# A one-core transformer layer with 32 experts on Trainium2: three embedding tiles computed in plain float32 beside the routing, the weights of experts 2 and 3 loaded behind the first two gathers, gate and up weights in 4 KB runs

## The chip, the core and the metric

The kernel runs on one core of a Trainium2 chip. The metric is the device time of one execution in microseconds, as the median of several runs. Engines are named as in the profile: PE is TensorE, ACT ScalarE, DVE VectorE, POOL GpSimd, SP SyncE; SPq and POOLq are the issuing of DMAs by the last two.

## The reference, cut to what matters

One layer over 1024 tokens of 1024 features in float32. What the change touches is the part from the router on:

```python
x = x + concat([attn_out, ml_out]) @ w_o                     # mixers, output projection
x = x + _hier_moe(_rmsnorm(x, norm_ffn_g), ...)              # 32 experts, each token in 2 of them
hp = _rmsnorm(x, norm_ple_g)
x = x + (p @ w_ple) * sigmoid(hp @ w_ple_gate)               # p: 1024 x 256, w_ple: 256 x 1024
return _rmsnorm(x, final_norm_g)

# in _hier_moe, for the rows xb of one expert e (w_g, w_u: 1024 x 256; w_d: 256 x 1024):
(silu(xb @ w_g[e]) * (xb @ w_u[e])) @ w_d[e]
```

The product `p @ w_ple` depends on inputs alone, so it can be computed at any time before the last stage; it is the "embedding" of the text.

## The kernel before, in words

Tokens are cut into 8 tiles of 128. First come the mixers (0 to some 430 us), then `out_tile` for each tile: output projection (`wops`), the residual `xres`, the normalised rows `h`, their transposes (`h2p`, `h2t`) and router logits (`rps`). `h` and `xres` are stored to DRAM by POOL (`h2d`, `x2d`). `route_tiles` and `route_static` turn the logits on DVE into positions, counts (`cnt`) and a table (`tab`) that holds for each expert the rows to gather (`gidx`) and to scatter (`sidx`).

The expert loop (`experts`) goes over 32 experts. For each: a gather of its rows by indirect DMA on POOL (`xg`, filled ahead by ACT, `moe_setup` L1200), transposes (`xgp`), a split of them in two parts (`xh` on ACT, `xl` on DVE), 24 matmuls against gate and up (`gups`), their product (`eh`), its transposes (`ehp`, `eht`), 12 matmuls against down (`eyps`), and an indirect scatter (`ybd`). Nearly all products are made in three passes (`mm3`, L127 to L129) from operands that `split` cuts in a high and a low part, ACT writing the one (L132) and DVE the other (L133).

Expert weights are 3 MB each, as three transfers of 1 MB into a ring of raw slots (`R`, `rring`), two of gate and up (`rgu`, each as a gate and an up DMA of 512 KB, `load_gu`) and one of down (`rdn`, `load_dn`); then they are split into a second ring (`W`, `wring`). SP issues them in program order, and each waits until its slot is free. Experts 0 and 1 are loaded during `out_tile`, expert 2 at the end of it on SP, the gate and up of expert 3 on POOL around the first two gathers.

An embedding tile (`ple_tile`) takes a 128 x 256 piece of `p` (`pin`, loaded by `ple_in` on SP one or two experts ahead), transposes it (`pps`), splits it (`eht`), makes 12 matmuls of 512 columns (`pleps`) and two copies by ACT into the tile's result. Six tiles are made in the expert loop, at the experts in `PLE_AT`; their results lie in raw slots that `retire` takes out of the ring. Tile 6 comes behind the last expert in `final_load`, ahead of a loop for overflowing experts that is passed without work here, tile 7 behind that loop in `final`, which adds everything up.

A scheduler sets the order of the instructions on each engine from the program's order, dependences and priorities.

Of the kernel before, what the change touches and what calls it, by code (L numbers as in the profile page):

```python
# [20 lines left out]
P = 128  # L21
# [18 lines left out]
PLE_AT = (14, 16, 18, 20, 22, 24)  # L40
# [19 lines left out]
class Kernel:  # L60
# [64 lines left out]
    def mm3(self, out, w_hi, w_lo, m_hi, m_lo, start, stop):  # L125
# [3 lines left out]
        nc.tensor.matmul(out, w_lo, m_hi, start=False, stop=stop)  # L129
# [735 lines left out]
    def out_tile(self, i, gb, before):  # L865
# [14 lines left out]
        def mm(c, lo_k, hi_k):  # L880
            s = slice(c * 512, (c + 1) * 512)
            for k in range(lo_k, hi_k):
                self.mm3(ps[c], hi[:, k], lo[:, k], self.wo[k][:, 0, s], self.wo[k][:, 1, s], k == 0, k == KT - 1)
# [226 lines left out]
    def load_gu(self, e, b, q=None):  # L1110
        raw = self.R("rgu")
        v = raw.rearrange("p (k u f) -> p k u f", k=4, u=2)
        for u, n in enumerate(("w_gate_e", "w_up_e")):
            w = self.weight(n, e).rearrange("(p k) f -> p k f", k=KT)
            (q or self.nc.sync).dma_start(v[:, :, u, :], w[:, 4 * b:4 * b + 4, :])
        return raw

    def load_dn(self, e):
        raw = self.R("rdn")
        self.nc.sync.dma_start(raw, self.weight("w_down_e", e).rearrange("(p k) n -> p (k n)", k=2))  # L1120
        return raw
# [21 lines left out]
    def split_gu(self, raws):  # L1143
        return [(h[:, o:o + 512], l[:, o:o + 512]) for h, l in self.split_w(raws) for o in (0, 512)]
# [58 lines left out]
    def experts(self, gu3):  # L1203
        col = lambda t, e: t[:, e:e + 1]
        xg = [self.moe_gather(col(self.gidx, e)) for e in range(2)]
        with self.tc.issue_after(self.gathered.ins):
            self.raws[3] = gu3, self.load_gu(3, 1, self.nc.gpsimd), self.load_dn(3)
        x, gu, h, dn = {0: self.moe_x(xg[0])}, {0: self.first[0]}, {}, {0: self.first[1]}
        for e in range(N_EXP + 1):
# [24 lines left out]
            if e in PLE_AT:  # L1234
                self.ple_tile(PLE_AT.index(e))
            if e + 1 in PLE_AT[1:]:
                self.ple_in(PLE_AT.index(e + 1))

# [15 lines left out]
    def final_load(self):  # L1254
# [6 lines left out]
        for i in range(len(PLE_AT), NT):  # L1261
# [5 lines left out]
        with self.tc.issue_after(sa), self.tc.issue_after(sv):  # L1267
            self.wring, self.nw = wr, 0
            self.wgs = self.split_gate(raws[:1], 0)
            self.ple_tile(len(PLE_AT))  # L1270
            self.wgs += self.split_gate(raws[1:3], 2)
        self.rest = wr, raws[3:]
# [6 lines left out]
    def ple_load(self):  # L1279
# [3 lines left out]
        self.ple_in(0)  # L1283
# [17 lines left out]
    def ple_tile(self, i):  # L1301
# [7 lines left out]
        n = i - len(PLE_AT)  # L1309
        if n >= 0:  # L1310
            y = self.t("B", "pley", [P, D], bufs=2, tag="ey") if n % 2 else self.t("B", "pley", [P, D], tag=f"xg{n // 2 % 2}")
        else:
            if i % 2 == 0:
                pool, tag = self.retire()
                self.ples = self.t(pool, "ples", [P, 2 * D], tag=tag)
            y = self.ples[:, i % 2 * D:(i % 2 + 1) * D]
# [51 lines left out]
    def final(self):  # L1368
# [12 lines left out]
        rest = list(range(len(PLE_AT) + 1, NT))  # L1381
# [40 lines left out]
    def run(self):  # L1422
# [13 lines left out]
        for i in range(NT):  # L1436
            end = self.out_tile(i, gb, end)
            if i == 1:
# [62 lines left out]
```

## Time and profile before

| | us |
|---|---|
| median of 3 runs (1030.44 to 1032.11) | 1030.52 |
| the profiled execution | 1031.45 |
| its span in the profile | 1029.7 |
| mixers, about | 0 to 430 |
| `out_tile` and the routing behind it | 430 to 564 |
| expert loop, first `gups` to last `eyps` | 564 to 909 |
| last stage | 909 to 1029.7 |

The profiled execution has 1.75 us outside its span and its mean granted PE clock is 0.966. A row of the timeline has the start, the length, engine, line, operation, output and inputs, a count where several were merged, and in brackets how long the engine had been idle and what released it. Matmul lengths overlap, so the spacing is read from the starts.

### The profile page before, as it was taken

The numbers are of one execution on the slowest core, as the hardware profiler recorded it, in microseconds if no ns is written. First come the engines' busy times: TensorE is split into PE (matmuls) and PEld (weight loads), VectorE is DVE, ScalarE is ACT, GpSimd is POOL, SyncE is SP. The second block draws the span as 40 slices with busy tenths as digits, with TensorE's granted clock in tenths as the row PEclk, the third lists the DMA queues.
The fourth block names the chain that finished last, engine by engine and source line by source line (L and its number), as shares of the span: only waits on it lengthen the run. The fifth ranks groups of instructions, "written<-read, shape, count | busy, mean of one in ns | idle before, by whom it ended". The sixth has DMA issues, their size and how long they took to land. (4 is left out here: it accounts for less than half of the span.)

```text
span 1029.7 us, 16040 instructions
## 1 busy us (share of the span) xinstructions
PE 953.9 (93%) x5583; PEld 819.2 (80%) x5583; DVE 805.8 (78%) x1877; ACT 666.7 (65%) x1182; POOL 165.7 (16%) x213
## 2 busy tenths in 40 slices
PE   4999999998999999899995989999699999979996
PEld 4999999996788888688884867888588888858875
DVE  7759788367888989774747899998678889858885
ACT  5554766254788889763333877998578788755432
POOL 4000000101222322101013121222112112210000
PEclk9999999999999999899996998999899999989999
DMA  7230111310000001698348898999999999774541
GB/s 220 101 101 25 42 62 59 102 37 11 17 11 14 13 12 23 229 295 288 123 159 272 261 359 283 354 351 343 338 301 315 341 304 356 243 254 173 184 164 61
DMA packets 127360, 185.36 MB, mean 180 GB/s; under 512 B 19487, under 2 KB 105070, under 8 KB 123182
## 3 DMA queue, kind: packets, MB, share of 16 engines
q1 hardware_dynamic: 111502, 146.00, 42.4%
q0 software_dynamic: 15776, 38.33, 10.4%
q8 instruction: 44, 0.72, 0.3%
q14 instruction: 38, 0.31, 0.1%
HBM read 167.48 MB, written 33.59 MB: 195 GB/s over the span
## 5 line engine op out<-in xcount | busy, mean ns | idle before, releaser
L133 DVE TENSOR_TENSOR w<-rgu,w 128x1024 fp32r<-128x1024 f32 x128 | 155.1, 1227 | 32.8 <-ACT w L132 29.6
L132 ACT ACTIVATE w<-rgu 128x1024 fp32r<-128x1024 f32 x128 | 133.3, 1065 | 6.1 <-PE gups L129 3.3
L127 PE MATMUL inp<-hh,win 128*128 128x256 f32 x384 | 111.7, 291 | 0.0
L129 PE MATMUL inp<-hh,win 128*128 128x256 f32 x384 | 111.1, 290 | 0.5 <-DVE win L256 0.5
L128 PE MATMUL inp<-hl,win 128*128 128x256 f32 x384 | 111.4, 291 | 0.1
L127 PE MATMUL gups<-w,xh 128*128 128x512 f32 x256 | 103.8, 405 | 0.0
L128 PE MATMUL gups<-w,xh 128*128 128x512 f32 x256 | 102.0, 398 | 0.0
L129 PE MATMUL gups<-w,xl 128*128 128x512 f32 x256 | 101.2, 395 | 0.0
L133 DVE TENSOR_TENSOR w<-rdn,w 128x1024 fp32r<-128x1024 f32 x64 | 77.2, 1219 | 2.7 <-ACT w L132 1.9
L129 PEld LDWEIGHTS inp<-hh,win 128*128 128x128 f32 x384 | 74.6, 195 | 0.7 <-DVE win L256 0.7
L128 PEld LDWEIGHTS inp<-hl,win 128*128 128x128 f32 x384 | 74.6, 194 | 0.5 <-DVE hl L133 0.4
L127 PEld LDWEIGHTS inp<-hh,win 128*128 128x128 f32 x384 | 74.5, 194 | 0.3 <-ACT z L331 0.2
L132 ACT ACTIVATE w<-rdn 128x1024 fp32r<-128x1024 f32 x64 | 66.0, 1067 | 4.1 <-PE gups L129 3.7
L1149 POOL DMA_INDIRECT xg<-h2d,gidx x32 | 37.1, 1159 | 179.2 <-PE xgp L1159 145.8
L1188 ACT ACTIVATE ey<-eyps 128x512 f32<-128x512 f32 x64 | 38.2, 596 | 40.4 <-PE eyps L129 30.8
L705 PE MATMUL po<-pt,V 128*128 128x256 f32 x320 | 61.2, 307 | 0.9 <-ACT pt L132 0.5
L133 DVE TENSOR_TENSOR pt<-ptp,pt 128x512 fp32r<-128x512 f32 (+2 forms) x112 | 54.3, 491 | 7.3 <-ACT pt L132 5.7
L132 ACT ACTIVATE pt<-ptp 128x512 fp32r<-128x512 f32 (+2 forms) x112 | 48.1, 443 | 14.7 <-PE ptp L693 7.4
L127 PE MATMUL eyps<-w,eht 128*128 128x512 f32 x128 | 54.5, 426 | 2.4 <-ACT eht L132 2.3
L129 PEld LDWEIGHTS gups<-w,xl 128*128 128x128 f32 x256 | 48.3, 189 | 9.5
L128 PEld LDWEIGHTS gups<-w,xh 128*128 128x128 f32 x256 | 48.6, 190 | 9.1
L127 PEld LDWEIGHTS gups<-w,xh 128*128 128x128 f32 x256 | 48.7, 190 | 9.0 <-ACT xh L132 0.2
(392 smaller groups left out, 2633.2 us busy)
## 6 DMA issues: line engine op xcount, KB each, us to landing
rdn<-in_w_down_e_dram SPq DMA_DIRECT2D x32, 1024.0 KB, 8.9
rgu<-in_w_gate_e_dram SPq DMA_DIRECT2D x62, 512.0 KB, 11.5
rgu<-in_w_up_e_dram SPq DMA_DIRECT2D x62, 512.0 KB, 10.0
wraw<-in_w_in_dram SPq DMA_DIRECT2D x11, 512.0 KB, 5.4
x<-in_x_dram SPq DMA_DIRECT2D x8, 512.0 KB, 4.6
abw<-mlrows SPq DMA_DIRECT2D x8, 512.0 KB, 3.7
mixf<-mixd SPq DMA_DIRECT2D x8, 512.0 KB, 5.7
xres<-in_x_dram SPq DMA_DIRECT2D x8, 512.0 KB
```

The costliest lines, as they stand in the source:

```text
L127: nc.tensor.matmul(out, w_hi, m_hi, start=start, stop=False)
L128: nc.tensor.matmul(out, w_hi, m_lo, start=False, stop=False)
L129: nc.tensor.matmul(out, w_lo, m_hi, start=False, stop=stop)
L132: a = self.nc.scalar.activation(hi, src, AF.Copy)
L133: v = self.nc.vector.tensor_sub(lo, src, hi)
L705: nc.tensor.matmul(po, self.V[kt][:, h, :], pts[t - 1][:, w, u, :], start=(kt + w == 0), stop=(kt == 2 * j + 1 and w == 1))
L1149: self.gathered = self.nc.gpsimd.indirect_dma_start(out=xg, out_offset=None, in_=self.h2d, in_offset=bass.IndirectOffsetOnAxis(ap=gcol, ax ...
L1188: nc.scalar.activation(y[:, s], py[c], AF.Copy)
```

## The change

- Of the small edits left out of the diff, one keeps the last `wops` matmul as `last_out`. `early_in` loads `w_ple` as it is (1 MB) into a raw slot after the first `out_tile`; `early_p` loads the first three pieces of `p`; `early_tile` makes three embedding tiles in plain float32, without a split: 2 transposes, one ACT copy, 4 matmuls of 512 columns, two ACT copies, and a store of the result to DRAM by SP. They are issued behind the last `wops` matmul at a low priority. The result of the third lies in a slot of `xres`, which later is a slot of `W`.
- No embedding tile is left in the expert loop. At expert 26 `ple_back` loads the three results back into two retired raw slots. Tiles 3, 4 and 5 come in `final_load`, ahead of the overflow loop, tiles 6 and 7 in `final`.
- `load_gu` writes gate and up as 4 KB runs; before, runs of 1 KB alternated. `split_gu` reads and writes pieces of 256 elements, so that `W` holds what it held before.
- The loads of expert 2 and of expert 3 go on POOL's queue behind the first two gathers. The order of the raw ring shifts by one.

```diff
@@ -37 +37 @@
 MLPRI = 800
 PLE_LOAD = 5
 PLE_W = (7, 9)
-PLE_AT = (14, 16, 18, 20, 22, 24)
+N_EARLY = 3
+PLE_BACK = 26
 MAGIC = 12582912.0
 TWO_PI = 2.0 * math.pi
 C1 = 6.28125
...
@@ -1108 +1110 @@
         return w[e] if isinstance(e, int) else w[bass.ds(e, 1)].rearrange("o k f -> (o k) f")
     def load_gu(self, e, b, q=None):
         raw = self.R("rgu")
-        v = raw.rearrange("p (k u f) -> p k u f", k=4, u=2)
         for u, n in enumerate(("w_gate_e", "w_up_e")):
             w = self.weight(n, e).rearrange("(p k) f -> p k f", k=KT)
-            (q or self.nc.sync).dma_start(v[:, :, u, :], w[:, 4 * b:4 * b + 4, :])
+            (q or self.nc.sync).dma_start(raw[:, u * D:(u + 1) * D].rearrange("p (k f) -> p k f", k=4),
+                                          w[:, 4 * b:4 * b + 4, :])
         return raw
-    def load_dn(self, e):
+    def load_dn(self, e, q=None):
         raw = self.R("rdn")
-        self.nc.sync.dma_start(raw, self.weight("w_down_e", e).rearrange("(p k) n -> p (k n)", k=2))
+        (q or self.nc.sync).dma_start(raw, self.weight("w_down_e", e).rearrange("(p k) n -> p (k n)", k=2))
         return raw
     def split_w(self, raws):
...
@@ -1141 +1144 @@
         return out
     def split_gu(self, raws):
-        return [(h[:, o:o + 512], l[:, o:o + 512]) for h, l in self.split_w(raws) for o in (0, 512)]
+        out = []
+        side = lambda t: t.rearrange("p (k u f) -> p u k f", k=2, u=2)
+        for raw in raws:
+            v = raw.rearrange("p (u k f) -> p u k f", u=2, k=4)
+            for j in range(2):
+                hi, lo = self.W("w")
+                self.last_split = self.split(side(hi), side(lo), v[:, :, 2 * j:2 * j + 2, :])
+                out += [(hi[:, o:o + 512], lo[:, o:o + 512]) for o in (0, 512)]
+        return out
     def moe_gather(self, gcol):
         xg = self.xgs[self.ngather % len(self.xgs)]
...
@@ -1200 +1212 @@
             self.nc.scalar.activation(x.rearrange("p (k n) -> p k n", k=KT),
                                       self.io_f.unsqueeze(1).to_broadcast([P, KT, P]), AF.Copy)
-    def experts(self, gu3):
+    def experts(self):
         col = lambda t, e: t[:, e:e + 1]
         xg = [self.moe_gather(col(self.gidx, e)) for e in range(2)]
         with self.tc.issue_after(self.gathered.ins):
-            self.raws[3] = gu3, self.load_gu(3, 1, self.nc.gpsimd), self.load_dn(3)
+            g = self.nc.gpsimd
+            self.raws[2] = self.load_gu(2, 0, g), self.load_gu(2, 1, g), self.load_dn(2, g)
+            self.raws[3] = self.load_gu(3, 0, g), self.load_gu(3, 1, g), self.load_dn(3)
         x, gu, h, dn = {0: self.moe_x(xg[0])}, {0: self.first[0]}, {}, {0: self.first[1]}
         for e in range(N_EXP + 1):
             if e + 2 < N_EXP:
...
@@ -1231 +1245 @@
                 self.ple_load()
             if e in PLE_W:
                 self.ple_weights(PLE_W.index(e))
-            if e in PLE_AT:
-                self.ple_tile(PLE_AT.index(e))
-            if e + 1 in PLE_AT[1:]:
-                self.ple_in(PLE_AT.index(e + 1))
+            if e == PLE_BACK:
+                self.ple_back()
     def overflow(self):
         nc, tc = self.nc, self.tc
...
@@ -1258 +1270 @@
         rr, wr = turn(self.rring, self.nr), turn(self.wring, self.nw)
         rr, wr = rr[:6], wr + rr[6:]
         raws = [self.R("rpg") for _ in range(4)]
-        for i in range(len(PLE_AT), NT):
+        for i in range(N_EARLY, NT - 1):
             self.ple_in(i)
         for k, t in enumerate(raws[:3]):
             with self.tc.issue_after(self.scats[N_EXP - (4, 3, 3)[k]].ins):
...
@@ -1267 +1279 @@
         with self.tc.issue_after(sa), self.tc.issue_after(sv):
             self.wring, self.nw = wr, 0
             self.wgs = self.split_gate(raws[:1], 0)
-            self.ple_tile(len(PLE_AT))
+            self.ple_tile(N_EARLY)
+            self.ple_in(NT - 1)
             self.wgs += self.split_gate(raws[1:3], 2)
+            self.ple_tile(N_EARLY + 1)
+            self.ple_tile(N_EARLY + 2)
         self.rest = wr, raws[3:]
         self.fin = {}
         self.rring, self.nr = rr[5:6], 0
...
@@ -1280 +1295 @@
         self.plew = []
         self.ple_raw = [self.ple_half(0)]
         self.pin, self.pw = {}, {}
-        self.ple_in(0)
+    def early_in(self):
+        self.early_w = self.R("rple")
+        self.nc.sync.dma_start(self.early_w, self.a["w_ple"][0].rearrange("(p k) n -> p (k n)", k=2))
+    def early_p(self):
+        self.early_x = self.t("A3", "pins", [P, N_EARLY, DE], tag="mixf")
+        self.nc.sync.dma_start(self.early_x, self.a["p"][0, 0, 0:N_EARLY * P, :].rearrange("(i p) n -> p i n", p=P))
+        self.pled = [self.t("dr", f"pled{i}", [P, D]) for i in range(N_EARLY)]
+    def early_tile(self, i):
+        nc = self.nc
+        pt = self.pT("pps")
+        for k in range(2):
+            nc.tensor.transpose(pt[:, k, :], self.early_x[:, i, k::2], self.ident)
+        ht = self.t("A3", "pht", [P, 2, P], F32, 2, "mixl")
+        nc.scalar.activation(ht, pt[:, 0:2], AF.Copy)
+        py = self.po2("pleps")
+        y = self.t("A3", "pley", [P, D], F32, 2, "xres" if i == 2 else "mixh")
+        for c in range(2):
+            s = slice(c * 512, (c + 1) * 512)
+            for k in range(2):
+                nc.tensor.matmul(py[c], ht[:, k], self.early_w[:, k * D + c * 512:k * D + c * 512 + 512], start=(k == 0),
+                                 stop=(k == 1))
+            nc.scalar.activation(y[:, s], py[c], AF.Copy)
+        nc.sync.dma_start(self.pled[i], y)
+    def ple_back(self):
+        self.ples = []
+        for n in range(2):
+            pool, tag = self.retire()
+            t = self.t(pool, "ples", [P, 2, D], tag=tag)
+            for i in range(2):
+                if 2 * n + i < N_EARLY:
+                    self.nc.sync.dma_start(t[:, i], self.pled[2 * n + i])
+                    self.pw[2 * n + i] = t[:, i]
+            self.ples = t[:, 1]
     def ple_in(self, i):
         self.pin[i] = self.t("B", "pin", [P, DE], bufs=4, tag="eh")
...
@@ -1306 +1360 @@
         ht = self.t("B", "eht", [P, 2, 2, P], F32R, 2)
         self.last_h = self.split(ht[:, 0], ht[:, 1], pt[:, 0:2])
         py = self.po2("pleps")
-        n = i - len(PLE_AT)
-        if n >= 0:
-            y = self.t("B", "pley", [P, D], bufs=2, tag="ey") if n % 2 else self.t("B", "pley", [P, D], tag=f"xg{n // 2 % 2}")
+        n = i - N_EARLY
+        if n == 0:
+            y = self.ples
+        elif n % 2:
+            y = self.t("B", "pley", [P, D], tag=f"xg{n // 2 % 2}")
         else:
-            if i % 2 == 0:
-                pool, tag = self.retire()
-                self.ples = self.t(pool, "ples", [P, 2 * D], tag=tag)
-            y = self.ples[:, i % 2 * D:(i % 2 + 1) * D]
+            y = self.t("B", "pley", [P, D], bufs=2, tag="ey")
         for c in range(2):
             s = slice(c * 512, (c + 1) * 512)
             for k in range(2):
...
@@ -1378 +1431 @@
             nc.sync.dma_start(t.rearrange("p (k n) -> p k n", k=2),
                               self.a["w_ple_gate"][0].rearrange("(k p) n -> p k n", p=P)[:, k:k + 2, :])
             self.final_in(1)
-        rest = list(range(len(PLE_AT) + 1, NT))
+        rest = list(range(N_EARLY + 3, NT))
         with ExitStack() as st:
             if rest:
                 self.ple_tile(rest.pop(0))
...
@@ -1435 +1488 @@
         end = None
         for i in range(NT):
             end = self.out_tile(i, gb, end)
+            if i == 0:
+                self.early_in()
             if i == 1:
                 self.raws[0] = self.moe_load(0)
+                self.nr += 1
             if i == 4:
                 list(self.route_tiles(0, 4))
                 self.first = self.split_gu(self.raws[0][:2]), self.split_w(self.raws[0][2:])
...
@@ -1446 +1502 @@
         next(rt)
         end()
         list(rt)
-        gu2 = self.load_gu(2, 0)
+        self.early_p()
+        with self.tc.issue_after(self.last_out.ins), self.tc.high_priority(-2000):
+            for i in range(N_EARLY):
+                self.early_tile(i)
         self.close("A3")
         list(self.route_tiles(7, 8))
         self.route_static()
         self.open("R2", "left")
         self.open("B", "left")
-        self.rring, self.nr = [("R2", f"R{i}") for i in range(4, 9)] + [self.rring[(self.nr + i) % 4] for i in range(4)], 0
+        self.rring, self.nr = [("R2", f"R{i}") for i in range(4, 9)] + self.rring, 0
         more = [("B", f"W{i}") for i in range(6, 9)]
         self.wring += more[:NW - 6]
         self.rring[5:5] = more[NW - 6:]
-        self.raws[2] = gu2, self.load_gu(2, 1), self.load_dn(2)
         self.moe_setup()
-        with self.tc.issue_after(self.stored.ins):
-            gu3 = self.load_gu(3, 0, self.nc.gpsimd)
         with self.tc.issue_after(self.routed.ins):
             self.route_rest()
-        self.experts(gu3)
+        self.experts()
         self.n_over = self.nc.values_load(self.nov[0:1, 0:1], min_val=0, max_val=15)
         self.final_load()
         self.overflow()
```

What stands on ACT at the end of the routing, before (`gd` and `e` belong to the routing weights, `xh` to the first experts' rows):

```order
L911 ACTIVATE h_6162<-h_6162,r_6165 128x512
L911 ACTIVATE h_6163<-h_6163,r_6165 128x512
L1200 ACTIVATE xg_6431<-io_f 128x1024
L1200 ACTIVATE xg_6432<-io_f 128x1024
L1031 ACTIVATE gd<-gd 128x32
L1037 ACTIVATE e_6445<-e_6445 128x8
L132 ACTIVATE w<-rgu 128x1024 x3
L132 ACTIVATE xh<-xgp 128x512 x4
L132 ACTIVATE w<-rgu 128x1024 x3
```

And in the changed program, with tile numbers (`pht` is an early tile's copy of the transposes, `pley` its two result copies):

```order
L1316 ACTIVATE pht_6358<-pps_6355 128x256
L1324 ACTIVATE pley_6362<-pleps_6360 128x512
L913 ACTIVATE h2_6164<-h2_6164,r2_6167 128x512
L913 ACTIVATE h2_6165<-h2_6165,r2_6167 128x512
L1324 ACTIVATE pley_6362<-pleps_6361 128x512
L1316 ACTIVATE pht_6373<-pps_6370 128x256
L1316 ACTIVATE pht_6388<-pps_6385 128x256
L1324 ACTIVATE pley_6377<-pleps_6375 128x512
L1324 ACTIVATE pley_6377<-pleps_6376 128x512
L1033 ACTIVATE gd_6479<-gd_6479 128x32
L1039 ACTIVATE e21_6486<-e21_6486 128x8
L1324 ACTIVATE pley_6392<-pleps_6390 128x512
L1324 ACTIVATE pley_6392<-pleps_6391 128x512
L1212 ACTIVATE xg0_6475<-io_f_81 128x1024
L1212 ACTIVATE xg1_6476<-io_f_81 128x1024
L133 ACTIVATE w_6579<-rgu_6038 128x2x2x256
L133 ACTIVATE w_6582<-rgu_6038 128x2x2x256
L133 ACTIVATE w_6585<-rgu_6041 128x2x2x256
L133 ACTIVATE xh_6516<-xgp_6518 128x512
```

The two fills of `xg` stood right behind `h`; now five `pley` copies, two of `pht`, `gd` and `e` stand between `h` and them, and one more `pley` copy stands ahead of `h`.

PE in the same place of the changed program (`pins` is the loaded piece of `p`, `rple` the loaded `w_ple`; before, `cnt` stood right behind the last `rps`, and `xgp` behind the last `tab`):

```order
L1314 MATMUL pps<-ident,pins 128x128 x2
L901 MATMUL rps<-wr,h2t 128x36 x4
L1322 MATMUL pleps<-rple,pht 128x512 x4
L1314 MATMUL pps<-ident,pins 128x128 x4
L1322 MATMUL pleps<-rple,pht 128x512 x2
L972 LDWEIGHTS upper
L972 MATMUL cnt<-M,upper 128x32
```

Behind the last `rps` stand one and a half early tiles, then `cnt`, then 14 of the 16 `tab` products, and between and behind the last two of them the rest:

```order
L1013 MATMUL tab<-Boh,Aoh 128x96
L1322 MATMUL pleps<-rple,pht 128x512
L1013 LDWEIGHTS Aoh
L1013 MATMUL tab<-Boh,Aoh 128x96
L1013 LDWEIGHTS Aoh
L1013 MATMUL tab<-Boh,Aoh 128x96
L1322 MATMUL pleps<-rple,pht 128x512 x5
L1171 MATMUL xgp<-ident,xg_6475 128x128 x8
```

SP in the changed program, from the load of `pins` on, with the semaphores that each waits for (`pled` is the store of an early tile):

```order
L1306 DMA pins<-in_p_dram 128x3x256 [waits DMAHW3_49,DVE_49]
L873 DMA xres<-in_x_dram 128x1024 [waits DMASW3_49,DMAHW2_49,PE_49,Activation_49]
L1325 DMA pled_6352<-pley 128x1024 [waits Activation_49]
L1325 DMA pled_6353<-pley 128x1024 [waits Activation_49]
L1123 DMA rdn<-in_w_down_e_dram 128x2048 [waits PE_49]
L1325 DMA pled_6354<-pley 128x1024 [waits Activation_49]
L1117 DMA rgu<-in_w_gate_e_dram 128x1024 [waits DVE_49]
```

The third store stands behind `rdn`, which waits for PE; the loads behind them start with expert 4.

POOL in the changed program:

```order
L916 DMA x2d<-xres 128x1024
L1161 DMA xg_6475<-h2d,gidx 128x1024
L1161 DMA xg_6476<-h2d,gidx 128x1024
L1117 DMA rgu<-in_w_gate_e_dram 128x1024
L1117 DMA rgu<-in_w_up_e_dram 128x1024
L1117 DMA rgu<-in_w_gate_e_dram 128x1024
L1117 DMA rgu<-in_w_up_e_dram 128x1024
L1123 DMA rdn<-in_w_down_e_dram 128x2048
L1117 DMA rgu<-in_w_gate_e_dram 128x1024
L1117 DMA rgu<-in_w_up_e_dram 128x1024
L1117 DMA rgu<-in_w_gate_e_dram 128x1024
L1117 DMA rgu<-in_w_up_e_dram 128x1024
L1161 DMA xg_6475<-h2d,gidx 128x1024
```

Before, only two loads stood ahead of the two gathers and two behind them; now nine stand between them and the third gather.

## Rows read from the trace of the kernel before

**Rows 1.** The page, busy time of each engine in us, its share of the span and its number of instructions.

```profile
PE 953.9 (93%) x5583; PEld 819.2 (80%) x5583; DVE 805.8 (78%) x1877; ACT 666.7 (65%) x1182; POOL 165.7 (16%) x213
```

**Rows 2.** Windows of 25 us: length, busy us of each engine (and its instructions), granted PE clock, DMA share, GB/s.

```profile
550.00:575.00 25.00, 14.20 (x75) 11.67 (x76) 18.14 (x62) 14.73 (x21) 10.17 (x12) 0.66 0.76 246
575.00:600.00 25.00, 25.00 (x123) 20.80 (x122) 24.07 (x29) 22.64 (x32) 5.46 (x4) 1.00 0.89 304
600.00:625.00 25.00, 19.74 (x96) 15.70 (x95) 22.90 (x59) 15.11 (x22) 5.05 (x5) 0.80 0.95 326
...
700.00:725.00 25.00, 25.00 (x124) 20.60 (x122) 21.75 (x24) 21.43 (x33) 6.52 (x6) 1.00 1.01 346
725.00:750.00 25.00, 16.99 (x67) 13.35 (x66) 12.47 (x16) 11.41 (x18) 2.03 (x2) 0.80 0.97 341
...
850.00:875.00 25.00, 25.00 (x122) 20.60 (x120) 23.34 (x26) 22.34 (x34) 6.07 (x6) 1.00 1.02 357
...
900.00:925.00 25.00, 18.61 (x75) 13.84 (x74) 12.97 (x16) 13.36 (x21) 3.85 (x4) 0.86 0.72 244
```

**Rows 3.** Timeline of PE, the transposes `ehp` of some experts.

```profile
711.81 0.39 PE L1179 MATMUL ehp<-ident,eh 128*128 128x128 f32 x2
...
724.33 0.39 PE L1179 MATMUL ehp<-ident,eh 128*128 128x128 f32 x2
...
734.63 0.39 PE L1179 MATMUL ehp<-ident,eh 128*128 128x128 f32 x2
...
757.28 0.39 PE L1179 MATMUL ehp<-ident,eh 128*128 128x128 f32 x2
...
766.81 0.39 PE L1179 MATMUL ehp<-ident,eh 128*128 128x128 f32 x2
...
779.36 0.39 PE L1179 MATMUL ehp<-ident,eh 128*128 128x128 f32 x2
...
788.88 0.39 PE L1179 MATMUL ehp<-ident,eh 128*128 128x128 f32 x2
...
845.55 0.39 PE L1179 MATMUL ehp<-ident,eh 128*128 128x128 f32 x2
...
855.08 0.39 PE L1179 MATMUL ehp<-ident,eh 128*128 128x128 f32 x2
```

**Rows 4.** Timeline of SP, the load of `pin`, and of PE, from the wait on.

```profile
729.90 4.23 SPq L1287 DMA_DIRECT2D pin<-in_p_dram  x1
...
742.51 0.67 PE L1305 MATMUL pps<-ident,pin 128*128 128x128 f32 x2 [7.49 <-DMA pin<-in_p_dram]
742.84 0.77 PE L127 MATMUL gups<-w,xh 128*128 128x512 f32 x1
743.41 0.63 PE L128 MATMUL gups<-w,xh 128*128 128x512 f32 x1
...
748.56 0.39 PE L127 MATMUL eyps<-w,eht 128*128 128x512 f32 x1
```

**Rows 5.** Timeline of PE in the mixers: plain float32 products with 128 columns, and what follows them.

```profile
109.47 1.06 PE L454 MATMUL mlp<-xc,w_mk 128*128 128x128 f32 x8
110.36 1.08 PE L458 MATMUL mlv<-w_mv,xm 128*128 128x128 f32 x8
```

**Rows 6.** Timeline of PE at the end of the routing.

```profile
547.64 1.08 PE L899 MATMUL rps<-wr,h2t 128*128 128x36 f32 x8 [0.75 <-ACT h2t L895]
554.49 0.21 PE L970 MATMUL cnt<-M,upper 128*128 128x32 bf16 x1 [5.77 <-DVE M L967]
...
554.57 1.68 PE L1011 MATMUL tab<-Boh,Aoh 128*128 128x96 bf16 x16
562.46 1.95 PE L1159 MATMUL xgp<-ident,xg 128*128 128x128 f32 x8 [6.21 <-DMA xg<-h2d,gidx]
564.24 0.79 PE L127 MATMUL gups<-w,xh 128*128 128x512 f32 x1
```

**Rows 7.** Timeline of ACT at the end of the routing.

```profile
549.94 1.33 ACT L911 ACTIVATE h<-h,r 128x512 f32<-128x512 f32 x2 [2.35 <-DVE r L109]
551.18 1.99 ACT L1200 ACTIVATE xg<-io_f 128x1024 f32<-128x1024 f32 x2
557.06 0.23 ACT L1031 ACTIVATE gd<-gd 128x32 f32<-128x32 f32 x1 [3.89 <-DVE gd L1030]
...
557.29 2.93 ACT L132 ACTIVATE w<-rgu 128x1024 fp32r<-128x1024 f32 x3
```

**Rows 8.** Timeline of POOL (a load, the first gather) and of SP (loads of expert 2) there.

```profile
552.66 0.77 POOL L1115 DMA_DIRECT2D rgu<-in_w_gate_e_dram  x1
...
557.84 1.10 POOL L1149 DMA_INDIRECT xg<-h2d,gidx  x1 [3.67 <-DVE e21d L1039]
...
540.23 0.38 SPq L1115 DMA_DIRECT2D rgu<-in_w_gate_e_dram  x1
...
541.27 2.49 SPq L1120 DMA_DIRECT2D rdn<-in_w_down_e_dram  x2
```

**Rows 9.** DMA totals of 660 to 720 us and of 426 to 437 us; then, of the page and of 545 to 575 us, issues by line: KB each and the median us to landing.

```profile
DMA packets 14372, 20.93 MB, mean 349 GB/s; under 512 B 1441, under 2 KB 12883, under 8 KB 13617
...
DMA packets 1502, 4.48 MB, mean 408 GB/s; under 512 B 111, under 2 KB 451, under 8 KB 1501
...
rdn<-in_w_down_e_dram SPq DMA_DIRECT2D x32, 1024.0 KB, 8.9
...
x2d<-xres POOLq DMA_DIRECT2D x1, 512.0 KB, 3.9
```

**Rows 10.** Timeline of PE at the end of the expert loop and the start of the last stage.

```profile
909.19 0.39 PE L129 MATMUL eyps<-w,eht 128*128 128x512 f32 x1
909.45 0.50 PE L127 MATMUL pleps<-wp,eht 128*128 128x512 f32 x1
...
916.75 0.70 PE L1305 MATMUL pps<-ident,pin 128*128 128x128 f32 x2 [4.17 <-issue]
...
922.74 0.60 PE L1363 MATMUL fp<-ident,fxy 128*128 128x128 f32 x4
```

**Rows 11.** The page, the costliest group of DVE (out<-in, count, busy us, mean ns), and the instructions of tile `eht` on DVE (ns min/median/max).

```profile
L133 DVE TENSOR_TENSOR w<-rgu,w 128x1024 fp32r<-128x1024 f32 x128 | 155.1, 1227 | 32.8 <-ACT w L132 29.6
...
L133 DVE TENSOR_TENSOR eht<-ehp,eht x32: 413/416/425, 579.6 to 906.5; 128x256 fp32r<-128x256 f32 x32
```

More of the change, by code (lines that the diff above doesn't have):

```diff
@@ L128, in mm3 @@
         nc.tensor.matmul(out, w_hi, m_lo, start=False, stop=False)
-        nc.tensor.matmul(out, w_lo, m_hi, start=False, stop=stop)
+        return nc.tensor.matmul(out, w_lo, m_hi, start=False, stop=stop)
     def split(self, hi, lo, src):
@@ L882, in mm @@
             for k in range(lo_k, hi_k):
-                self.mm3(ps[c], hi[:, k], lo[:, k], self.wo[k][:, 0, s], self.wo[k][:, 1, s], k == 0, k == KT - 1)
+                self.last_out = self.mm3(ps[c], hi[:, k], lo[:, k], self.wo[k][:, 0, s], self.wo[k][:, 1, s], k == 0,
+                                         k == KT - 1)
         def norm(c):
```

## The prediction

> **What bounds the kernel now.** I read the busy times first, then the table of 25 us windows, then the starts of the expert loop, and last the two stretches in which TensorE (PE) rests. PE is busy for 953.9 of 1029.7 us, VectorE (DVE) for 805.8 and ScalarE (ACT) for 666.7 [rows 1]: PE is the first suspect. The windows say where it holds: from 575 on nearly every window has 25.00 us of PE in 25 at a granted clock of 1.00, and the gaps are few: 550–575 with 14.20, 600–625 with 19.74, 725–750 with 16.99 and 900–925 with 18.61 [rows 2]. So in the expert loop an instruction taken off PE shortens the span, and the four gaps are the only places where work on PE can be free.
>
> **The embedding tiles that leave the loop.** The transposes `ehp` mark one expert each. From 779.36 to 788.88 and from 845.55 to 855.08 an expert without an embedding tile takes 9.52 us; from 711.81 to 724.33 and from 766.81 to 779.36, with a tile, 12.52 and 12.55 [rows 3]. The difference, 3.0 us, is the price of a tile where PE is full. Six tiles leave the loop: 6 x 3.0 = **18.0 us less**.
>
> **The wait for an input tile.** Between 734.63 and 757.28 lie 22.65 us instead of 12.55 [rows 3]. The tile's transposes wait 7.49 us for the transfer of `pin`, and the thirteen or so matmuls after them start 0.43 us apart instead of 0.23, until 748.56 [rows 4]. That is the lower of the clock's two levels, 1.2 GHz: the window's mean is 0.80 [rows 2]. SyncE issued that load at 729.90, taking 4.23 us, among expert weights of up to 1 MB [rows 4]. The changed loop holds no such tile, so wait and cold matmuls go: 22.65 - 12.55 = **10.1 us less**. Late next would be an expert's weights, which have a ring of several experts' depth where `pin` had one tile's; the windows of 25.00 on both sides say that this ring was in time.
>
> **What the three early tiles cost.** A plain float32 product shows as two records per matmul: `mlp` with 128 columns puts 8 records, 4 matmuls, between 109.47 and 110.36, 0.22 us for each [rows 5]. A matmul of 512 columns is then an estimated 0.9 us, a tile of four 3.6, the three tiles 10.7 us and some 0.8 of transposes. They go into a stretch where PE rests 5.77 us (until 554.49, for DVE's routing arithmetic) and 6.21 us (until 562.46, for the gather) [rows 6]: 12 us of cover for 11.5 of work. If the cover held wholly the cost would be nothing, and that is the low end. I do not believe it, because of the order on the engines around it. I follow it by durations:
> - PE: tile 0 from 548.7 (the end of the last `rps`) to 552.4; tile 1's first half waits for its ACT copy, which stands behind the two `h` scalings, and ends near 555.3. Only then `cnt`, which before ran at 554.49 [rows 6]: +0.9. After 14 of the 16 `tab` matmuls one early matmul comes in between, so the gather's indices are some 1.8 us late. The other five end near 562.4.
> - ACT: the two fills of `xg` ran before at 551.18, well ahead of need, and the gather at 557.84 [rows 7, 8]. Now they stand behind the last `pley` copy, near 563.1, and take 1.99 us together [rows 7]; the first gather goes out near 564.1, 6.3 us later than before. Its landing took from 557.84 to 562.46, 4.6 us [rows 6, 8], so `xgp` starts near 568.7.
> - The three weight splits that ran at 557.29 (2.93 us) stand on ACT ahead of `xh` [rows 7], and the first of them now waits until the third tile's store has left the buffer under it. The store is issued near 563.1, behind a 1 MB `rdn`; alone such a store takes 3.9 us and the `rdn` 8.9 [rows 9]. It lands between 567 and 572, the splits end between 570 and 575, and the first `gups`, at 564.24 before [rows 6], comes between 570.3 and 575.6.
>
> Cost 6 to 11.5 us by this, 0 if the order did not matter; I take **7 us more**, the near end, since the store is half the size of the `rdn` and both have the queues almost alone. Before, ACT rested 3.89 us ahead of `gd` with work behind it [rows 7]; no row shows it passing an instruction that waits. The Trainium skill's page "TensorE: Matmul & The Clock Gate", section "Architectural detail: the array is 16× 32×32, not 1× 128×128", says that ScalarE and VectorE work strictly in order, and only TensorE pulls weight loads forward. By that rule the fills cannot pass the copies and the sum keeps its 7 us; were it not so, it would be 0 to 3 and the time 1006 to 1009.
>
> Expert 2's weights came before from 540.23 on (its `rdn` at 541.27 on SyncE) and now come through GpSimd's queue behind the two gathers, with expert 3's: 6 MB. An issue there costs 0.77 us [rows 8]; the nine issues end near 572 and at the 349 GB/s of a full stretch [rows 9] 6 MB need 18 us, so expert 2 is in by 578 and expert 3 by 585. Expert 2's first matmuls come two paces, 19 us, after 571. I cost this at nothing; the cover is those 19 us.
>
> **The end.** Before, tile 6 follows the last `eyps` at 909.19, PE rests 4.17 us until the program's loop for overflow is passed, then tile 7 runs on the low clock until 922.74 [rows 10]: 13.3 us from tile 6's start at 909.45. Now three tiles stand before that loop and two behind it, 15.1 us at 3.0 each if the rest vanishes, 19.3 if all of it stays: +1.8 to +6.0. The first three end near 918.6 on the old scale, later than the loop was passed before, so most of the rest is covered; I take **3 us more**.
>
> **The 4 KB runs.** They move the same bytes. Where gate and up come in 1 KB runs a full stretch moves 349 GB/s (12883 of 14372 packets under 2 KB); where most packets are larger, 408 [rows 9]. As PE is the bound I give this no gain; it matters as a reserve, below. The read-back of three tiles, 1.5 MB, is 4 us of queue time late in the loop: nothing.
>
> **Sum.** The profiled execution took 1031.45 us, its span 1029.7, and it is 0.9 us above the median of the three runs (1030.52). 1031.45 - 18.0 - 10.1 + 7 + 3 = 1013.35, rounded to **1013 us**. By the low ends 1005.2 (0 and 1.8), by the high ends 1020.9 (11.5 and 6).
>
> **Rivals.**
> - The loads become the bound. The windows from 575 to 900 move 104 MB, and about 28 experts' weights, 3.15 MB each, are loaded in them; with the rows gathered and scattered that is 3.6 MB an expert, and at 9.52 us a pace of 376 GB/s. A full stretch gave 349 [rows 9]. At 349 an expert takes 10.3 us, and from the gathers near 566 the 30 experts from the third on need 308 us, until 874, about when PE would come to the last of them: nothing to spare, after a head start now one expert shorter. Any idle queue time then lengthens the span; I put 5 to 13 us: 1018 to 1026, with another late transfer in the place of `pin` as its sign. Against it stand the 408 GB/s. The page "DMA: Bandwidth & Descriptors" of the Trainium skill, section "Where 436 GB/s comes from", has about 358 GB/s of HBM binding loads into SBUF; by that, 10.1 us an expert, the longer runs could not help and this rival would be right. The 408 of the trace is above that figure.
> - The routing gap hides the early tiles: 1006 (0 in place of the 7 there). For it 12 us of rest against 11.5 of work, against it the order on ACT.
> - **Slower than before**: the split of gate and up now reads and writes runs of 256 elements in four pieces. DVE is 23.34 of 25 us busy in a window at the pace of 9.52 [rows 2], 8.9 us an expert, four splits of 1.227 among it [rows 11]. A split 0.3 us longer makes DVE's expert 10.1 us, and over 31 experts that eats 18 us, all that is gained; from there on DVE decides. The low bound is no change. The high one: from 256 to 1024 elements an instruction goes from 0.416 to 1.227 us [rows 11], so 0.15 us is its fixed part; were that paid for each of four runs, a split would take 0.44 more, DVE's expert 10.65, and the time 1013 + 31 x 1.1 = 1048. I take no change, as nothing in the rows ties the fixed part to a run. The page "Vector Engine (DVE) Microarchitecture Reference", section 5.2, says that hops are free between runs of two words or more; by that this rival falls. No run shown so far has such a split.
> - The change does not do what it says: the 10.1 us were an accident of one execution, or a new wait of that size takes its place. Then 1023.
>
> **How the numbers follow.** Forecast (1005 to 1018) 0.61; loads as the bound 0.13; routing hidden 0.08; a new wait of 10 us 0.07; DVE as the bound 0.06; a gain eaten by several of these to within 0.2%, which is about what a measurement here can tell from no change, 0.03. For a price of the early tiles above 25 us, which would also be slower, 0.02. Faster is the sum of the first four, 0.89; same 0.03; slower 0.06 + 0.02 = 0.08. The range from 1005 to 1025 leaves out the DVE rival, part of the supply rival and the lowest corner.
>
> **What would show it.** Right: `ehp` 9.5 us apart through the loop but for the old gap near 611; no `pin` wait; the first `gups` near 571, after a rest of PE before `xgp`, with ACT waiting at the first `w<-rgu` for a DMA. Wrong: the split's mean on DVE above 1.5 us; PE waiting for ACT's splits and these for `rgu`, at a DMA share of 1.0; a first `gups` past 580.

## The result, and the profile after

The changed kernel takes 1045.12 us (median of 4, 1043.4 to 1048.0) against 1030.98 for the kernel before: ratio 1.0134, interval [1.0116, 1.0152]. It is slower by 14 us, where 17.5 us faster was predicted. The profiled execution took 1045.14, its span 1043.4 us.

The page of the changed kernel, busy time and DMA packets, and its windows of 25 us (columns as in [rows 2]):

```profile
PE 960.5 (92%) x5571; PEld 818.0 (78%) x5571; DVE 803.6 (77%) x1874; ACT 666.7 (64%) x1182; POOL 169.3 (16%) x218
...
DMA packets 80720, 189.56 MB, mean 182 GB/s; under 512 B 19567, under 2 KB 41662, under 8 KB 76414
```

```profile
575.00:600.00 25.00, 17.74 (x73) 14.73 (x74) 13.96 (x16) 12.86 (x16) 3.06 (x3) 0.77 0.87 339
...
725.00:750.00 25.00, 24.64 (x118) 20.05 (x118) 22.62 (x25) 21.90 (x32) 6.97 (x6) 1.00 0.98 365
750.00:775.00 25.00, 23.26 (x114) 18.80 (x113) 21.29 (x26) 18.85 (x28) 4.92 (x5) 1.00 0.99 346
775.00:800.00 25.00, 23.32 (x111) 18.66 (x110) 20.85 (x24) 20.64 (x30) 7.32 (x6) 1.00 1.01 373
...
825.00:850.00 25.00, 22.13 (x98) 17.75 (x98) 20.51 (x23) 17.74 (x25) 4.73 (x4) 0.93 0.96 355
```

Where [rows 2] had 25.00 us of PE from 575 to 600, there is now a hole. From 750 to 850, where the kernel before had 25.00 in each window, PE now rests in every one, at a DMA share of 0.96 to 1.01. The share alone says little: from 700 to 725 it was 1.01 before, with PE at 25.00 [rows 2]. The wait at 742 of [rows 4] is gone, as it should be.

Four marks split the difference: the first `gups`, the first and the last `ehp`, and the end of the span.

| | before | after | change | predicted |
|---|---|---|---|---|
| first `gups` | 564.24 | 573.09 | +8.85 | +7 |
| to the first `ehp` | 14.38 | 24.33 | +9.95 | 0 |
| first to last `ehp` | 326.82 | 315.75 | -11.07 | -28.1 |
| last `ehp` to the end | 124.26 | 130.23 | +5.97 | +3 |

They add to +13.70, the difference of the spans.

The routing end, for comparison with [rows 6 to 8], first on ACT, then on POOL and PE of the changed kernel:

```profile
562.36 0.60 ACT L1324 ACTIVATE pley<-pleps 128x512 f32<-128x512 f32 x1 [1.12 <-PE pleps L1322]
562.85 1.99 ACT L1212 ACTIVATE xg<-io_f 128x1024 f32<-128x1024 f32 x2
569.61 2.95 ACT L133 ACTIVATE w<-rgu 128x1024 fp32r<-128x1024 f32 x3 [4.76 <-issue]
```

```profile
564.18 1.10 POOL L1161 DMA_INDIRECT xg<-h2d,gidx  x1 [9.32 <-ACT xg L1212]
...
576.17 1.04 POOL L1161 DMA_INDIRECT xg<-h2d,gidx  x1 [1.93 <-PE xgp L1171]
```

```profile
570.28 1.94 PE L1171 MATMUL xgp<-ident,xg 128*128 128x128 f32 x8 [7.96 <-DMA xg<-h2d,gidx]
573.09 0.79 PE L128 MATMUL gups<-w,xh 128*128 128x512 f32 x1 [0.87 <-ACT xh L133]
...
594.63 1.94 PE L1171 MATMUL xgp<-ident,xg 128*128 128x128 f32 x8 [7.26 <-DMA xg<-h2d,gidx]
```

The first gather goes out at 564.18 (forecast: 564.1). The splits on ACT start at 569.61, after a wait of 4.76 us whose releaser the row doesn't name; the forecast had them wait for the third tile's store, and `a_bare` below bears that out. The **third** gather, issued at 576.17, is used at 594.63, 18.5 us later, with PE idle for 7.26 us of it and then at a lower clock (mean 0.77 in that window). Between it and the first two, POOL had issued 5 MB of weights: eight loads of 512 KB and one of 1 MB. The prediction counted 6 MB, but the down weights of expert 3 stay on SP.

The loop: the group that splits gate and up on ACT (count, busy, mean ns, idle time before it by releaser), from 560 to 910 us, of the kernel before and of the changed one:

```profile
L132 ACT ACTIVATE w<-rgu 128x1024 fp32r<-128x1024 f32 x122 | 127.4, 1066 | 6.1 <-PE gups L129 3.3 <-DMA rgu<-in_w_up_e_dram 2.8
```

```profile
L133 ACT ACTIVATE w<-rgu 128x1024 fp32r<-128x1024 f32 x124 | 128.5, 1064 | 40.1 <-DMA rgu<-in_w_up_e_dram 28.9 <-issue 4.8 <-PE gups L130 2.7
```

ACT waits 28.9 us for weights instead of 2.8. The split itself did not slow down (1064 against 1066 ns, on DVE 1225 against 1227 of [rows 11]): the rival that put DVE in the way falls at once.

### The profile page after: what moved, and what is told of

The parts are those of the page before. It is cut to its first block, busy times and chain, and to the rows that moved or that the text cites. A ratio compares the mean times of both kernels' runs of the same rounds, so it can differ in the third digit from the quotient of the medians.

```text
span 1043.4 us, 16007 instructions
## 1 busy us (share of the span) xinstructions
PE 960.5 (92%) x5571; PEld 818.0 (78%) x5571; DVE 803.6 (77%) x1874; ACT 666.7 (64%) x1182; POOL 169.3 (16%) x218
## 5 line engine op out<-in xcount | busy, mean ns | idle before, releaser
L134 DVE TENSOR_TENSOR w<-rgu,w 128x1024 fp32r<-128x1024 f32 x128 | 153.8, 1225 | 40.4 <-ACT w L133 38.1
L133 ACT ACTIVATE w<-rgu 128x1024 fp32r<-128x1024 f32 x128 | 132.6, 1064 | 40.1 <-DMA rgu<-in_w_up_e_dram 28.9
L1161 POOL DMA_INDIRECT xg<-h2d,gidx x32 | 39.2, 1224 | 229.1 <-PE xgp L1171 169.1
L1171 PE MATMUL xgp<-ident,xg 128*128 128x128 f32 x256 | 42.1, 293 | 18.8 <-DMA xg<-h2d,gidx 15.2
L1171 PEld LDWEIGHTS xgp<-ident,xg 128*128 128x128 f32 x256 | 38.1, 195 | 24.2 <-issue 16.6
L128 PEld LDWEIGHTS gups<-w,xh 128*128 128x128 f32 x256 | 48.6, 190 | 10.4 <-ACT xh L133 1.5
```

The lines of the kernel that those rows point to most:

```text
L128: nc.tensor.matmul(out, w_hi, m_hi, start=start, stop=False)
L133: a = self.nc.scalar.activation(hi, src, AF.Copy)
L134: v = self.nc.vector.tensor_sub(lo, src, hi)
L1161: self.gathered = self.nc.gpsimd.indirect_dma_start(out=xg, out_offset=None, in_=self.h2d, in_offset=bass.IndirectOffsetOnAxis(ap=gcol, ax ...
L1171: self.nc.tensor.transpose(pt[:, k, :], xg[:, 4 * b + k::KT], self.ident)
```

## The experiments

Two theories stood after the comparison. **Supply**: in the loop the weights come at a rate that PE at 9.52 us an expert outruns, so what is taken off PE there comes back as waits. **Start**: the loop only suffers from beginning late and an expert short of loaded weights. For the first hole: **queue**, the third gather stands behind the weights in POOL's queue. All rows below are medians and ratios to the kernel before, which was timed again beside each group of runs (medians of 1031.2 to 1032.15 us); the marks are from one profiled execution each. `b_bare`, `a_half` and `a_bare` leave work out and so compute something else.

| | us | ratio [95%] | first `gups` | first `ehp` | first to last `ehp` |
|---|---|---|---|---|---|
| `b_bare` | 1021.67 | 0.9911 [0.9886, 0.9936] | 564.07 | 578.36 | 315.0 |
| `b_runs` | 1032.24 | 1.0004 [0.9989, 1.0020] | 563.62 | 578.47 | 325.6 |
| `b_pin` | 1026.64 | 0.9955 [0.9929, 0.9981] | 563.03 | 577.67 | 321.6 |
| `a_sp` | 1043.05 | 1.0114 [1.0098, 1.0131] | 574.39 | 589.12 | 317.9 |
| `a_half` | 1026.08 | 0.9941 [0.9920, 0.9962] | 570.32 | 593.88 | 296.2 |
| `a_bare` | 1038.59 | 1.0067 [1.0048, 1.0085] | 566.37 | 592.49 | 314.1 |
| `a_1k` | 1046.50 | 1.0146 [1.0129, 1.0163] | 572.81 | 593.37 | 319.8 |
| `b_pin_runs` | 1023.57 | 0.9912 [0.9896, 0.9929] | 564.05 | 580.35 | 318.3 |
| `b_pool` | 1041.13 | 1.0104 [1.0071, 1.0137] | 565.07 | 589.65 | 325.9 |
| `b_t11` | 1021.07 | 0.9900 [0.9867, 0.9932] | 565.42 | 581.24 | 315.4 |
| `b_t12s3` | 1024.09 | 0.9923 [0.9896, 0.9951] | 564.95 | 583.21 | 316.9 |
| `b_five` | 1021.59 | 0.9907 [0.9888, 0.9926] | 565.74 | 581.94 | 313.7 |

**`b_bare`**, the kernel before with no tile in its loop:

```diff
-            if e in PLE_AT:
-                self.ple_tile(PLE_AT.index(e))
-            if e + 1 in PLE_AT[1:]:
-                self.ple_in(PLE_AT.index(e + 1))
+            if e in PLE_AT[::2]:
...
+                self.nc.gpsimd.memset(self.ples, 1.0)
```

> The kernel before with the six embedding tiles of the expert loop and their input loads left out (their results are filled with ones by GpSimd). Theory supply: the weights come at about 360 GB/s whatever PE does, some 10.0 to 10.3 us an expert, so the loop cannot run at 9.52 us to its end; the gain is the wait for an input tile and a part of the 18 us, and the time is 1010 to 1018 us, with DMA share 1.0 and ACT waiting for gate and up weights late in the loop. Theory start (the loop of the changed kernel suffers only from its late and short start): nothing of that kind here, the full 28 us, 1003 us.

Six tiles and the 10 us wait, 28 us of PE's time, are taken away with nothing put in their place, at an unchanged start, and 9.6 us is all that comes of it. ACT waits 17.9 us for `rgu` in its loop, against 2.8 before. Start falls, since nothing at the start was changed; the sign of supply is there, though the time is 4 us above the upper end of what it expected. The loop is 315.0 us long, the changed kernel's 315.8. That the two are so near may be partly chance: this one starts with more weights in store and reads no results back, but has 345 GB/s (660 to 860 us) where the changed one has 361.

**`a_half`**, the changed kernel with half of each down weight:

```diff
-        (q or self.nc.sync).dma_start(raw, self.weight("w_down_e", e).rearrange("(p k) n -> p (k n)", k=2))
+        (q or self.nc.sync).dma_start(raw[:, 0:D], self.weight("w_down_e", e).rearrange("(p k) n -> p (k n)", k=2)[:, 0:D])
...
-                self.last_split = self.split(hi, lo, raw[:, k * D:(k + 1) * D])
+                self.last_split = self.split(hi, lo, raw[:, 0:D])
```

> The changed kernel with only one half of each down weight loaded, and split twice: 0.5 MB of some 3.6 MB an expert less to load, everything else as it is. Theory supply: at 360 GB/s an expert's bytes now take 8.7 us, less than PE's 9.52, so the loop runs at 9.52 us almost throughout and ACT's waits for gate and up weights go; first to last ehp some 300 us in place of 315.8, the time 1028 to 1032 us. If something else than the bytes holds the loop (the ring of slots, the order on ACT), nothing changes: 1043 to 1046.

With the same instructions on PE, ACT and DVE and half a megabyte less an expert, the loop runs at 9.5 us an expert but for the old gap near 611, 296.2 us in all, and the time falls by 19 us, 2 us further than expected. The wait of ACT for `rgu` goes from 28.9 to 3.1 us. The ring of slots and the order on ACT are as they were, so it is the bytes that hold the loop of the changed kernel:

```profile
L133 ACT ACTIVATE w<-rgu 128x1024 fp32r<-128x1024 f32 x124 | 128.5, 1065 | 9.3 <-issue 3.2 <-DMA rgu<-in_w_up_e_dram 3.1 <-PE gups L130 2.8
```

DMA totals from 660 to 860 us, each from its own kernel: before, changed, `a_half`, and `a_1k` (below):

```profile
DMA packets 46059, 65.74 MB, mean 329 GB/s; under 512 B 4292, under 2 KB 41503, under 8 KB 43885
```

```profile
DMA packets 19845, 72.17 MB, mean 361 GB/s; under 512 B 4711, under 2 KB 4711, under 8 KB 17377
```

```profile
DMA packets 21284, 66.79 MB, mean 334 GB/s; under 512 B 5011, under 2 KB 5011, under 8 KB 21270
```

```profile
DMA packets 47346, 69.60 MB, mean 348 GB/s; under 512 B 4637, under 2 KB 42186, under 8 KB 44919
```

`a_half` moves 66.79 MB in 200 us, 3.18 MB in 9.52 us; with the 0.52 left out an expert needs 3.70 MB. At 361 GB/s that is 10.25 us, at 348 it is 10.6. PE without tiles needs 9.52. The changed kernel runs at 9.5 from the `ehp` at 664.23 to the one at 740.28, on weights in store, and then at 10.3 until the one at 884.81. As the 361 GB/s were measured in the very loop that waits, this fit is no proof by itself; the proof is `a_half`.

**`a_bare`**, the changed kernel without the work of its early tiles (`early_tile` is not called; `ple_back` loads rows of `x`).

> The changed kernel without the work of the three early tiles (transposes, matmuls, copies, stores left out; rows of x are loaded in the place of their results). The difference of the first gups is the price of the tiles where they stand: by the prediction's step 6 to 11 us, from 573.1 back to 562 to 567. Theory supply: the loop gives part of it back as waits for weights, the time 1036 to 1042. Theory start: all of it stays, 1034 to 1037.

The first `gups` come 6.7 us earlier, inside the 6 to 11.5 that the prediction worked out for these tiles. The last `rps` comes 1.1 us later here (549.87 against 548.76), so counted from it the tiles cost 7.8 us: 24.3 us from there to the first `gups` with them, 16.5 without, 16.6 in the kernel before. Without the tiles and their stores the splits on ACT wait for nothing:

```profile
559.52 2.93 ACT L133 ACTIVATE w<-rgu 128x1024 fp32r<-128x1024 f32 x3
```

The time is 6.5 us less, in the range of supply and above that of start, but that is nearly all of the 6.7, and the marks of the one profiled execution are too few to say what the loop took back. Not settled by this run.

**`b_pool`**, before with only the move of the loads of experts 2 and 3 to POOL; **`a_sp`**, the changed kernel with these loads on SP (`g = self.nc.sync`).

> The kernel before with one part of the change alone: the weights of experts 2 and 3 on GpSimd's queue behind the first two gathers (in 1 KB runs, tiles in the loop, no early tiles). Theory queue: the third gather lands 15 to 18 us after its issue, behind 6 MB of the same queue, and the first ehp comes 8 to 10 us later, near 587. With PE as the bound behind it all of it reaches the end: 1038 to 1042 us; with the supply as the bound a part of it is taken from waits for weights, which also start with an expert less in store: 1034 to 1042. If the loads are hidden, as the prediction had it: 1031.

> The changed kernel with the weights of experts 2 and 3 issued by SyncE behind the first two gathers instead of by GpSimd. Theory queue: the gathers of experts 2 and 3 no longer stand behind 6 MB in GpSimd's queue and land 5 to 8 us after their issue instead of 18; the first ehp comes some 8 us earlier. How much of it is left at the end tells the bound of the loop: theory start 1036 us, theory supply 1038 to 1045, since the loop takes back what the start gains.

`b_pool` has the hole without early tiles or longer runs: third gather issued at 571.42, its transposes at 586.86, 15.4 us; first `ehp` 11.0 us later, and 9.8 us at the end. POOL and PE of `b_pool`, then of `a_sp`:

```profile
571.42 1.06 POOL L1149 DMA_INDIRECT xg<-h2d,gidx  x1 [1.59 <-DMA rgu<-in_w_up_e_dram]
...
586.86 1.94 PE L1159 MATMUL xgp<-ident,xg 128*128 128x128 f32 x8 [8.52 <-DMA xg<-h2d,gidx]
```

```profile
574.83 0.99 POOL L1161 DMA_INDIRECT xg<-h2d,gidx  x1 [8.00 <-PE xgp L1171]
...
582.69 1.12 PE L1171 MATMUL xgp<-ident,xg 128*128 128x128 f32 x8
```

In `a_sp` the same gather, issued at 574.83, keeps nobody waiting, and the first `ehp` is 8.3 us earlier. One edit makes the hole and the other takes it away: the queue is the cause. The gather shares the engines, too: from 578 to 590 the changed kernel moves 4.92 MB, of which only 2.56 on POOL's queue and the rest on SP's, for later experts. Of these 8.3 us the medians keep 2.1, as supply expects, but the profiled execution, the fastest of its four (1039.16), still has 6.2 of them at the last `ehp`: on the loop this run is inconclusive.

**`b_runs`**, before with the change's `load_gu` and `split_gu`; **`a_1k`**, the changed kernel with those of before.

> The kernel before with gate and up loaded in 4 KB runs and split from them, nothing else. Theory supply: the rate of a full stretch rises by no more than 5% (to about 360 GB/s), PE with its tiles needs hardly more than that, and the time stays within 5 us of before, 1026 to 1031, most of the change in the wait for the input tile. Theory runs (the longer runs or the split in pieces do harm): slower by 5 us or more.

> The changed kernel with gate and up in alternating runs of 1 KB as before, the rest as changed. Theory supply: a loop that waits for its weights feels the rate, 345 to 349 GB/s in place of 361, so each of the some 22 experts that wait costs 0.3 us more: 1048 to 1054. If the rate does not matter: 1045.

`b_runs` is before again, 1 us above the range of supply. In `a_1k` the loop grows by 4.0 us at 348 GB/s, but its first `ehp` comes 4.05 us earlier, the third gather being used at 590.79. So the runs are worth some 4 us where the loop waits for weights, less than expected and by one profiled execution of each, and here the start cancelled them. Why the gather passes sooner was not tried; the traces show that from 578 to 590 SP's queue, in runs of 1 KB, moves 1.49 MB there and POOL's 2.75, against 2.36 and 2.56 in the changed kernel.

**`b_pin`**, the input tiles two experts ahead, and **`b_pin_runs`**, that with the 4 KB runs:

```diff
-            if e + 1 in PLE_AT[1:]:
-                self.ple_in(PLE_AT.index(e + 1))
+            if e + 2 in PLE_AT[1:]:
+                self.ple_in(PLE_AT.index(e + 2))
```

> The kernel before with the input tiles of the embedding loaded two experts ahead instead of one. If the 10.1 us of the wait and its cold matmuls are paid by the end and the weights are in time: 1021 us. Theory supply: PE with its tiles needs 10.1 us an expert on average and the weights at 349 GB/s come each 10.3 us, so a part comes back as waits for weights: 1022 to 1027.

> The kernel before with the input tiles two experts ahead and the 4 KB runs. Theory supply: with the wait gone, PE and supply stand close (317.8 us from first to last ehp with 1 KB runs, some 316 by PE alone), so the longer runs give 1 to 4 us: 1022 to 1026. If packet size has no part in it: 1026.6.

The wait of [rows 4] goes with this one edit, and about half of its 10.1 us stays. `b_pin_runs` gains 9 us, with all six tiles in the loop, which at 318.3 us is 2.5 us longer than the changed kernel's with none.

**`b_t11`**, **`b_t12s3`**, **`b_five`**: that version with `PLE_AT` at 11, 13, ... 21; at 12, 15, ... 27; and at 11, 13, ... 19 with one tile more at the end.

> The kernel before with the 4 KB runs, the input tiles two experts ahead, and the six tiles at experts 11, 13, ... 21 instead of 14, 16, ... 24. Theory supply: the store of weights in the ring is used up by the experts without a tile ahead of the first one; tiles three experts earlier keep it from running dry, so ACT's waits for weights fall and the time is 1 to 3 us below the 1023.6 us of tiles at 14: 1021 to 1023. But the ring loses its three slots earlier too, and if that weighs more: 1024 to 1027.

> The same with the six tiles at every third expert, 12, 15, ... 27. Theory supply: the mean pace of an expert between 12 and 28 becomes 10.5 us, over the 10.0 that the supply allows, so ACT hardly waits for weights there, and the slots of the ring go later: 1021 to 1023. If the waits do not depend on the spacing: 1023.6.

> As the version with tiles at 11, 13, ... 21, 4 KB runs and input tiles two experts ahead, but the sixth tile moved from the loop to the end (one ahead of the overflow loop, two behind it). That version's loop waits for weights for 0.6 us only, so PE is its bound and the loop gets up to 3 us shorter as far as the supply allows; the end gets longer by the price of a tile there. By the changed kernel, whose end is 6 us longer with three tiles more, 2 us: 1020 to 1022 in place of 1021.1. If a tile behind the overflow loop costs its full 3 us and the supply takes the loop's gain: 1022 to 1024.

At 11 to 21 the tiles begin before the loaded weights run out; ACT's wait for `rgu` falls to 0.6 us, from 7.1 in `b_pin_runs`:

```profile
L132 ACT ACTIVATE w<-rgu 128x1024 fp32r<-128x1024 f32 x123 | 128.2, 1066 | 3.7 <-PE gups L129 3.2 <-DMA rgu<-in_w_up_e_dram 0.6
```

1021.07 us is the lowest median of all, 1.0% below the kernel before, and no more than `b_bare` takes without the six tiles. The intervals of the three placements overlap, so which of them is best isn't settled. Every third expert is no better than 14 to 24. `b_five` is even with `b_t11`: its loop is 1.6 us shorter and its end 1.0 us longer.

## Why the prediction was wrong

- **The tiles and the wait, -28.1 us predicted, -11.1 measured.** Both terms were sized rightly as PE's time (`a_half`, with the loop of the changed kernel and enough weights, runs it in 296.2 us, 30.6 less than before). The step that failed is the sentence on what is late next: "the windows of 25.00 on both sides say that this ring was in time". It was in time at a pace that tiles and the wait slowed to 326.8 us for 31 steps, 10.5 each. The pace of the changed loop had to be held against the supply, not the old one: an expert's weights take 10.3 us there, and 17.0 of the 28.1 us come back as waits for them.
- **The read-back, put at nothing, stands in these 17 us.** The prediction called it "4 us of queue time late in the loop". In the changed kernel SP issues it at 859.51, the next weights only at 867.50; ACT waits for them until 882.64, and one step of the loop takes 16.06 us, 6.5 too many:

```profile
859.51 3.92 SPq L1335 DMA_DIRECT2D ples<-pled  x3
...
882.64 1.06 ACT L133 ACTIVATE w<-rgu 128x1024 fp32r<-128x1024 f32 x1 [5.77 <-DMA rgu<-in_w_up_e_dram]
...
884.81 0.39 PE L1191 MATMUL ehp<-ident,eh 128*128 128x128 f32 x2
...
900.87 0.39 PE L1191 MATMUL ehp<-ident,eh 128*128 128x128 f32 x2
```

  The same step takes 15.8 to 16.4 us in `a_sp`, `a_bare` and `a_1k`, and 9.5 in `a_half`, which reads back as much but has bytes to spare. Two slots leave the ring at the same place; the two were not tried apart.
- **The rival that was right was priced too low and set aside.** It said 3.6 MB and 376 GB/s; 3.70 MB were measured, and its 5 to 13 us were 17. I gave it 0.13 because of the 408 GB/s in [rows 9]. That stretch loads, with other things, 1 MB blocks for the output projection; the loop with its longer runs reached 361. The Trainium skill's page "DMA: Bandwidth & Descriptors", section "Where 436 GB/s comes from", names about 358 GB/s. The loop's 361 is close to it, the 408 is not, nor is another stretch of the changed kernel, 575 to 595 us, mostly loads from two queues:

```profile
DMA packets 2191, 7.90 MB, mean 395 GB/s; under 512 B 391, under 2 KB 391, under 8 KB 2063
```

  The figure foretold this loop but is no ceiling; what holds the loop at 361 with the engines full was not isolated.
- **The loads on POOL, costed at nothing, were 10 us.** The step asked when the weights of experts 2 and 3 are needed, and its cover of 19 us was sized for them. It left out who stands behind them on that queue: the third gather. The Trainium skill's page "DMA: Bandwidth & Descriptors", section "Two DMAs through the same engine are not ordered", says that descriptors within a queue of a DMA engine start in order. The trace agrees: 18.5 us behind 5 MB, and no wait where the weights went by SP.
- **The early tiles, +7 predicted.** Right in its mechanism: gather at 564.18 for 564.1, splits ending at 572.6 for 570 to 575. +8.85 measured, of which 1.1 lies ahead of it (the last `rps` is at 548.76 instead of 547.64); the rest fits the 7.8 of `a_bare`.
- **The end, +3 predicted, +5.97 measured**, at the upper bound. The prediction took most of the old rest of 4.17 us as covered, but PE still rests 4.4: it waits 2.48 us for `eht`, ACT being busy with the split of the gate weights, and 1.94 us at the overflow loop:

```profile
923.07 0.50 PE L128 MATMUL pleps<-wp,eht 128*128 128x512 f32 x1 [2.48 <-ACT eht L133]
...
930.87 0.74 PE L1359 MATMUL pps<-ident,pin 128*128 128x128 f32 x4 [1.94 <-issue]
```

  This was read, not tested.
- **The range.** Slower had 0.08, most of it for DVE, which had no part in it. The true case was two rivals at once (the supply, 17 us in the loop, and a new wait of 10), which I had let come together only far enough to cancel the gain (0.03), never to make the kernel slower.

## What to carry to other kernels

A loop in which PE is busy in every window can still have its next bound a few per cent below: before taking work out, divide the bytes of one step by the rate of a full stretch of that same loop, and take the gain only down to that for the steps whose bytes are not yet in store. Work that fits between the two bounds is best left there, rather than paid for elsewhere: `b_t11`, with the longer runs and earlier input tiles, makes six tiles in its loop in the time that `b_bare` takes with none. When transfers change their queue, look at everything that is issued to that queue behind them, small indirect ones above all.

## What was not expected of the hardware

At a DMA share near 1.0 runs of four times the length raised the loop's rate from 348 to 361 GB/s only, 4%. And a gather of 128 rows at most took 18.5 us from issue to use behind 5 MB in its own queue, but under 8 us (574.83 to 582.69, PE not waiting) when the same 5 MB went by another queue, issued from 563.57 on instead of 566.60.
